# Squares of x written over the raw weight tiles, and two early loads of x issued from ScalarE's queue, in a one-core decoder step

## The chip, the cores and the metric

The kernel runs on one core of a Trainium2 chip. The time is the device time of one execution in microseconds (us); lower is better. A profile is one further execution, recorded by the hardware profiler. Its engines are called PE (TensorE, matmuls), PEld (PE's weight loads), DVE (VectorE), ACT (ScalarE), POOL (GpSimd) and SP (SyncE, which here only issues DMAs). "SPq" and "ACTq" are the sequencers of SP and ACT when they issue a DMA. L12 is line 12 of the kernel as it stood before the change.

## What is computed

One layer of a decoder, for 256 new prompt tokens and 8 x 4 sample tokens, which the kernel puts side by side as T = 288 columns. All data is 32-bit floating point.

```python
def trunk_layer(x, hist_conv, hist_pool, pos0, norm1_g, w_in, b_in, conv_w, conv_b,
                ln_g, ln_b, pool_w, pool_scale, w_out, norm2_g, w_ff1, w_ff2):
    h = rmsnorm(x, norm1_g)
    proj = jnp.einsum("btd,de->bte", h, w_in) + b_in
    a, gate, z = proj[..., :D_CONV], proj[..., D_CONV:2 * D_CONV], proj[..., 2 * D_CONV:]
    u = a * jax.nn.sigmoid(gate)
    ...
    c = jax.nn.silu(layernorm(depthwise_causal_conv(u_ext, conv_w, conv_b), ln_g, ln_b))
    ...
    d = multiscale_pool(z_ext, pos0)
    p = jnp.einsum("btgc,gce->btge", d, pool_w).reshape(bsz, T, D_POOL) * pool_scale
    x = x + jnp.einsum("btm,md->btd", jnp.concatenate([c, p], axis=-1), w_out)
    h2 = rmsnorm(x, norm2_g)
    f = jnp.square(jax.nn.relu(jnp.einsum("btd,df->btf", h2, w_ff1)))
    x = x + jnp.einsum("btf,fd->btd", f, w_ff2)
    return x, u_ext[:, -(CONV_W - 1):], z_ext[:, -(POOL_MAX - 1):]
```

The model width is 2048 (16 blocks of 128 channels), the hidden width of the MLP 8192, the convolution has 31 taps, the pooling windows are 2, 4, 8 and 16. A last rmsnorm follows. The change concerns the first rmsnorm and the first columns of the input projection.

## The kernel before the change

Channels lie on the 128 partitions and tokens along the free axis. x is the tile `xT`, 16 blocks of 128 x 288. Each 32-bit operand of a matmul is split into a high part (a rounded copy, made on ACT) and a low part (what is left, by a subtraction on DVE or POOL), and each product is three matmuls: high by high, high by low, low by high. Weights arrive as raw tiles of 128 x 1024 elements (512 KB); ACT copies one to `whi` (L250, in the first phase L339), and the subtraction gives `wlo` (L251, L340).

The raw tiles come from a pool of six buffers (L87). A tile's buffer goes to a later tile only when everything that reads or writes the earlier one is done. The first eight raw tiles (`first_raw`, L164) serve the first phase; all later ones are loaded by `load` (L154 to L162).

**The first phase** (L323 to L357) runs c from 0 to 7. Step c takes the channel blocks 2c and 2c+1 of x and the raw tile `first_raw[c]`, which holds these two blocks' weights for four groups of 128 output columns. ACT scales the blocks by the norm's gain (`hh`, L332), DVE makes the low part `hl` (L333), ACT and DVE split the weights (L339, L340), and PE does 24 matmuls into four accumulators (L346). c = 0 and c = 1 are done in two halves, one block each, so that they can begin with less data. The norm itself is left out of these products: its factor is a number per token, and is multiplied in behind them.

That factor needs the sum over channels of the squares of x. `square(c)` (L313) has ACT square the two blocks of step c and DVE add the result to a running sum (L318). Before the change the squares lie in a region of the tile `uz` that the pooled inputs `z` need only later. The code calls `square(c - 1)` at the end of step c for c = 1 to 6, and `square(6)`, `square(7)` and the last fold `tot` (L354) in the midst of step 7. Then PE adds over the channels (`token_sum`, L225), ACT takes a square root (L232) and loads the next function table (L208), DVE finishes the reciprocal, PE spreads it over the partitions (L242), and DVE copies it to `rb` (L360).

**Then** comes the next group of columns: 16 k-blocks by two accumulators, three matmuls each (L257 to L259), with four raw tiles of its own, whose low parts are made on POOL (L251). All later groups of the kernel have this form.

**The order of the work.** The program's text says what depends on what; which instruction stands where in each engine's own order is chosen by a planner when the program is built (L632). It may place an instruction ahead of others that come before it in the text. On the chip each engine then runs its instructions strictly in that order. The DMAs of the start are written out by hand (L177 to L196): the small `vec` on ACT, all others on SP, pieces of x and of weights in turn. SP waits where a load's buffer is not free yet, or where the load eight places earlier has not landed.

Of the kernel before, what the change touches and what calls it, by code (L numbers as in the profile page):

```python
# [12 lines left out]
ALU = mybir.AluOpType  # L13
# [7 lines left out]
T = SEQ + NB * NS  # L21
# [8 lines left out]
N8 = DC // P  # L30
# [4 lines left out]
UL = UO + NB * US  # L35
# [46 lines left out]
def trunk_kernel(ctx: ExitStack, tc: tile.TileContext, io):  # L82
    nc = tc.nc
# [14 lines left out]
    def nm(s):  # L98
        seen[s] = seen.get(s, 0) + 1
        return f"{s}{seen[s]}"  # L100
# [8 lines left out]
    def row(name):  # L109
        return rowp.tile([P, T], F32, name=nm(name), tag="row")  # L110
# [4 lines left out]
    def act(name, **kw):  # L115
        return slot(name, F32R, **(kw or {"tag": "act"}))

    def tmp(name, n=T, tag="tmp", bufs=6):
        return tmpp.tile([P, n], F32, name=nm(name), tag=tag, bufs=bufs)
# [10 lines left out]
    def f32(t):  # L130
        return t[:].bitcast(F32)
# [8 lines left out]
    xT = const.tile([P, KT, T], F32, name="xT")  # L140
    uz = const.tile([P, N8 * (UL + ZL)], F32, name="uz")
    u_all = uz[:, 0 : N8 * UL].rearrange("p (k t) -> p k t", t=UL)
    z_all = uz[:, N8 * UL :].rearrange("p (k t) -> p k t", t=ZL)
    squares = uz[:, N8 * UL : N8 * UL + 8 * T].rearrange("p (n k t) -> p n k t", k=2, t=T)

    def v(key, j):
        return vec[:, OFF[key] + j : OFF[key] + j + 1]
# [3 lines left out]
    def raw_tile():  # L151
        return wraw.tile([P, 4, 256], F32, name=nm("wr"), tag="wr")
# [10 lines left out]

    first_raw = [raw_tile() for _ in range(8)]  # L164

    def load_x(k, n):

        nc.sync.dma_start(xT[:, k : k + n, :], io["xT"][:, k : k + n, :])

    def load_first(c, k0=0, k1=2):  # L170

        to = first_raw[c][:].rearrange("p (b k) n -> p b k n", b=2)
        src = io["w"][2 * (c // 4) : 2 * (c // 4) + 2].rearrange("b p k n -> p b k n")
        at = 2 * (c % 4)
        nc.sync.dma_start(to[:, :, k0:k1, :], src[:, :, at + k0 : at + k1, :])

    nc.scalar.dma_start(vec[:, 0:CWO], io["vec"][:, 0:CWO])  # L177
    load_x(0, 1)
    load_first(0, 0, 1)
    load_x(1, 1)  # L180
    load_first(0, 1, 2)
    load_x(2, 2)
    load_first(1, 0, 1)
    load_first(1, 1, 2)
    load_x(4, 2)
# [36 lines left out]
    def token_sum(pt, t, first=True, last=True):  # L222

        for j in range(3):
            nc.tensor.matmul(pt[:TB, j : j + 1], t[:, j * TB : (j + 1) * TB], ones[:, 0:1], start=first and j == 0, stop=last and j == 2)  # L225
# [86 lines left out]

    def square(c):  # L313

        to = squares[:, 0] if c == 0 else squares[:, 1 + c % 3]
        nc.scalar.activation(to, xT[:, 2 * c : 2 * c + 2, :], AF.Square)  # L316
        if c:
            nc.vector.tensor_tensor(squares[:, 0], squares[:, 0], to, op=ALU.add)  # L318

    def lhs(t, k, m):  # L320
        return t[:, 2 * (m // 2) + k, (m % 2) * P : (m % 2 + 1) * P]

    for c in range(8):  # L323
        pair = []
        hi = wspl.tile([P, 4, 256], F32R, name=nm("whi"), tag="whi")
        lo = wspl.tile([P, 4, 256], F32R, name=nm("wlo"), tag="wlo")
        views = [t[:].rearrange("p (b k) n -> p b k n", b=2) for t in (first_raw[c], hi, lo)]
        steps = ((0, 1), (1, 2)) if c < 2 else ((0, 2),)
        for k0, k1 in steps:
            for k in range(2 * c + k0, 2 * c + k1):  # L330
                hh, hl = act("hh"), act("hl")
                nc.scalar.activation(hh, xT[:, k, :], AF.Copy, scale=v("norm1_g", k))  # L332
                nc.vector.scalar_tensor_tensor(out=hl, in0=xT[:, k, :], scalar=v("norm1_g", k), in1=f32(hh), op0=ALU.mult, op1=ALU.subtract)  # L333
                pair.append((hh, hl))
            if len(steps) == 2:
                r, h, l = [t[:, :, k0, :] for t in views]
            else:
                r, h, l = first_raw[c], hi, lo
            nc.scalar.copy(h, r)  # L339
            nc.vector.tensor_tensor(l, r, h.bitcast(F32) if len(steps) == 2 else f32(hi), op=ALU.subtract)  # L340
            for w, x in ((hi, 0), (hi, 1), (lo, 0)):
                if c == 7 and w is lo:
                    token_sum(total, rows[0])
                for k in range(k0, k1):
                    for m in range(4):
                        nc.tensor.matmul(  # L346
                            first_banks[m][:, :T], lhs(w, k, m), pair[k][x],
                            start=c == 0 and k == 0 and w is hi and x == 0, stop=c == 7 and k == 1 and w is lo,
                        )
                if c == 7 and w is hi and x == 0:  # L350
                    square(6)
                    square(7)
                    rows = [row("tot")]
                    nc.vector.tensor_tensor(rows[0], squares[:, 0, 0], squares[:, 0, 1], op=ALU.add)  # L354
        hx += pair
        if 0 < c < 7:
            square(c - 1)  # L357
    ready.extend(itertools.islice(weights, 1))
    rb = row("rb")
# [156 lines left out]
    for g in range(8):  # L516
        bk = bank2()
        gemm(bk, mixc)
        for m in range(2):
            k = 2 * g + m  # L520
# [18 lines left out]
    for ch in range(DFF // FCH):  # L539
        fx = []  # L540
        for g in range(FCH // 256):
# [4 lines left out]
            for m in range(2):  # L546
                t = tmp("t")
# [98 lines left out]
```

## Time and profile before

| | |
|---|---|
| three runs | 1082.31, 1082.53, 1083.08 us; median 1082.53 |
| the profiled execution | 1082.96 us, of which the program's span is 1081.2 |
| PE busy | 1066.8 us, 99% of the span |
| DVE, ACT, POOL busy | 630.5, 470.7, 162.6 us |
| granted TensorE clock, mean | 0.995 of full |
| read from HBM | 181.49 MB, 172 GB/s with the writes |

Each number of the table but the runs comes from the profile page, the execution's own time from its result. PE overlaps its matmuls, so that a busy PE need not be a PE at its peak. In rows of time, the first number is the start in us from the span's beginning and the second the length; "x4" counts instructions that were drawn together, and a bracket gives the idle time of that engine before the row and what ended it. In rows of a DMA, the last number is the time in us from issue to landing.

### The profile page before, as it was taken

Reading aid. Unit: us, or ns where it says so; the run is one execution under the profiler, and the core shown is the slowest. Engines: PE = TensorE matmul, PEld = TensorE weight load, DVE = VectorE, ACT = ScalarE, POOL = GpSimd, SP = SyncE. Lnnn points to the kernel's source line nnn. Section 1 sums busy time; section 2 is a strip of 40 time slices with the busy share of each in tenths; the row PEclk is TensorE's granted clock in tenths of the full one; section 3 lists DMA queues with packets and bytes.
Section 4 is the critical chain, followed back from the end, with each engine's and each line's share of the span. In section 5 each row is a group of like instructions: output and inputs, shape, how many; then the busy total and the mean of one; then the engine's idle time right before and its main releaser. Section 6 shows DMA issues by size and latency. Waiting matters only on the chain.

```text
span 1081.2 us, 19737 instructions
## 1 busy us (share of the span) xinstructions
PE 1066.8 (99%) x8186; PEld 1065.2 (99%) x8186; DVE 630.5 (58%) x982; ACT 470.7 (44%) x650; POOL 162.6 (15%) x108
## 2 busy tenths in 40 slices
PE   9999999999999999999999999999999999999995
PEld 9999999999999999999999999999999999999995
DVE  7799999687555444445455444455444455555453
ACT  7543554575544433334443333444433334444441
POOL 0899878500000000000000000000000000000000
PEclk9999999999999999999999999999999999999997
DMA  9755567555555555555555555555555555555522
GB/s 333 229 185 173 182 169 234 170 168 166 164 167 173 166 169 175 166 167 175 163 170 175 166 167 174 165 169 175 166 167 174 164 170 176 164 168 175 163 93 88
DMA packets 56649, 187.04 MB, mean 173 GB/s; under 512 B 5872, under 2 KB 11504, under 8 KB 56560
## 3 DMA queue, kind: packets, MB, share of 16 engines
q1 hardware_dynamic: 56416, 185.74, 54.8%
q8 instruction: 64, 1.05, 0.4%
q14 instruction: 25, 0.20, 0.1%
q10 hardware_dynamic: 144, 0.05, 0.0%
HBM read 181.49 MB, written 4.28 MB: 172 GB/s over the span
## 4 chain that ended last, share of the span: by engine, by line
PE 98%; DVE 1%; ACT 0%; DMA 0%; SPq 0%; DVEq 0%; issue 0%
PE ac L257 32%; PE ac L258 32%; PE ac L259 32%; PE ac L346 1%; PE cv L346 1%; DVE xT L586 0%; DMA xT<-in_xT 0%; PE pr L242 0%; ACT hh L332 0%; ACT uz L316 0%; PE pf L225 0%; ACT whi L339 0%; DVEq L632 0%; PE m L259 0%; PE m L258 0%
## 5 line engine op out<-in xcount | busy, mean ns | idle before, releaser
L250 ACT CAST whi<-wr 128x1024 fp32r<-128x1024 f32 x330 | 344.9, 1046 | 569.4 <-PE ac L258 542.6
L251 DVE TENSOR_TENSOR wlo<-wr,whi 128x1024 fp32r<-128x1024 f32 x272 | 333.2, 1225 | 366.1 <-ACT whi L250 366.1
L257 PE MATMUL ac<-ah,whi 128*128 128x288 f32 x1024 | 298.7, 292 | 0.0
L257 PE MATMUL ac<-fh,whi 128*128 128x288 f32 x1024 | 298.6, 292 | 0.0
L258 PE MATMUL ac<-al,whi 128*128 128x288 f32 x1024 | 298.5, 292 | 0.0
L259 PE MATMUL ac<-ah,wlo 128*128 128x288 f32 x1024 | 298.5, 291 | 0.0
L258 PE MATMUL ac<-fl,whi 128*128 128x288 f32 x1024 | 298.5, 291 | 0.0
L259 PE MATMUL ac<-fh,wlo 128*128 128x288 f32 x1024 | 298.5, 291 | 0.0
L257 PEld LDWEIGHTS ac<-ah,whi 128*128 128x128 f32 x1024 | 191.9, 187 | 0.0
L258 PEld LDWEIGHTS ac<-al,whi 128*128 128x128 f32 x1024 | 191.9, 187 | 0.0
L257 PEld LDWEIGHTS ac<-fh,whi 128*128 128x128 f32 x1024 | 191.9, 187 | 0.0
L258 PEld LDWEIGHTS ac<-fl,whi 128*128 128x128 f32 x1024 | 191.9, 187 | 0.0
L259 PEld LDWEIGHTS ac<-ah,wlo 128*128 128x128 f32 x1024 | 191.9, 187 | 0.0
L259 PEld LDWEIGHTS ac<-fh,wlo 128*128 128x128 f32 x1024 | 191.9, 187 | 0.0
L251 POOL TENSOR_TENSOR wlo<-wr,whi 128x1024 fp32r<-128x1024 f32 x58 | 138.3, 2403 | 21.3 <-ACT whi L250 19.5
L399 DVE SCALAR_TENSOR_TENSOR pc<-uz,vec,pc 128x256 f32<-128x256 f32 x232 | 98.9, 482 | 6.3 <-ACT pc L388 4.3
L257 PE MATMUL ac<-hh,whi 128*128 128x288 f32 x320 | 92.3, 292 | 0.8 <-ACT uz L420 0.8
L258 PE MATMUL ac<-hl,whi 128*128 128x288 f32 x320 | 92.1, 292 | 0.0
L259 PE MATMUL ac<-hh,wlo 128*128 128x288 f32 x320 | 87.4, 292 | 0.0
L257 PEld LDWEIGHTS ac<-hh,whi 128*128 128x128 f32 x320 | 60.0, 187 | 1.0 <-ACT uz L420 1.0
L258 PEld LDWEIGHTS ac<-hl,whi 128*128 128x128 f32 x320 | 59.9, 187 | 0.0
L259 PEld LDWEIGHTS ac<-hh,wlo 128*128 128x128 f32 x320 | 57.9, 187 | 0.0
(153 smaller groups left out, 872.0 us busy)
## 6 DMA issues: line engine op xcount, KB each, us to landing
wr<-in_w SPq DMA_DIRECT2D x336, 512.0 KB, 3.8
out_u_out<-uz SPq DMA_DIRECT2D x1, 1208.0 KB, 9.0
xT<-in_xT SPq DMA_DIRECT2D x2, 576.0 KB, 8.3
out_yT<-xT SPq DMA_DIRECT2D x2, 576.0 KB, 2.9
uz<-in_hist_c SPq DMA_DIRECT2D x1, 1088.0 KB, 12.3
wr<-in_w SPq DMA_DIRECT2D x4, 256.0 KB, 4.7
xT<-in_xT SPq DMA_DIRECT2D x3, 288.0 KB, 5.9
out_z_out<-uz SPq DMA_DIRECT2D x1, 668.0 KB, 10.2
```

Source lines behind the costliest of these rows:

```text
L250: nc.scalar.copy(hi[:, a:b, :], raw[:, a:b, :])
L251: eng.tensor_tensor(lo[:, a:b, :], raw[:, a:b, :], hi[:, a:b, :].bitcast(F32), op=ALU.subtract)
L257: nc.tensor.matmul(b, wh, xh, start=first, stop=False)
L258: nc.tensor.matmul(b, wh, xl, start=False, stop=False)
L259: nc.tensor.matmul(b, wl, xh, start=False, stop=last)
L346: nc.tensor.matmul(first_banks[m][:, :T], lhs(w, k, m), pair[k][x], start=c == 0 and k == 0 and w is hi and x == 0, stop=c == 7 and k == 1 ...
L399: nc.vector.scalar_tensor_tensor(out=dst, in0=u_all[:, i, w : w + SEQ], scalar=cw[i][:, w : w + 1], in1=pc[i], op0=ALU.mult, op1=ALU.add)
```

## The change

The running sum keeps a place in `uz`, now of 2 x 288 elements. The square of step c is written over the raw weights of step c, into the first 576 of the 1024 elements of `first_raw[c]`. The first square is not added by itself: the first addition takes the squares of c = 0 and c = 1 and writes the sum. The calls stand at the same places, except that `square(0)` takes its own place at the end of step 1. The loads of block 1 and of blocks 2 and 3 of x are issued by ACT in place of SP; their places in the text are the same.

```diff
-    squares = uz[:, N8 * UL : N8 * UL + 8 * T].rearrange("p (n k t) -> p n k t", k=2, t=T)
+    squares = uz[:, N8 * UL : N8 * UL + 2 * T].rearrange("p (k t) -> p k t", t=T)
...
-    def load_x(k, n):
+    def load_x(k, n, eng=nc.sync):
 
-        nc.sync.dma_start(xT[:, k : k + n, :], io["xT"][:, k : k + n, :])
+        eng.dma_start(xT[:, k : k + n, :], io["xT"][:, k : k + n, :])
...
     load_x(0, 1)
     load_first(0, 0, 1)
-    load_x(1, 1)
+    load_x(1, 1, nc.scalar)
     load_first(0, 1, 2)
-    load_x(2, 2)
+    load_x(2, 2, nc.scalar)
     load_first(1, 0, 1)
...
     def square(c):
 
-        to = squares[:, 0] if c == 0 else squares[:, 1 + c % 3]
+        to = first_raw[c][:].rearrange("p a b -> p (a b)")[:, 0 : 2 * T].rearrange("p (k t) -> p k t", t=T)
         nc.scalar.activation(to, xT[:, 2 * c : 2 * c + 2, :], AF.Square)
         if c:
-            nc.vector.tensor_tensor(squares[:, 0], squares[:, 0], to, op=ALU.add)
+            nc.vector.tensor_tensor(squares, first_square if c == 1 else squares, to, op=ALU.add)
+        return to
...
                     rows = [row("tot")]
-                    nc.vector.tensor_tensor(rows[0], squares[:, 0, 0], squares[:, 0, 1], op=ALU.add)
+                    nc.vector.tensor_tensor(rows[0], squares[:, 0], squares[:, 1], op=ALU.add)
         hx += pair
-        if 0 < c < 7:
+        if c == 1:
+            first_square = square(0)
+        elif 1 < c < 7:
             square(c - 1)
```

## The prediction

> **What bounds the kernel now.** I read the span, then the busy time of the engines by stretch, then what TensorE (PE) waits for, then the chain of work that ended last.
>
> ```profile
> span 1081.2 us, 19737 instructions
> ```
> ```profile
> 4.92:9.56 4.64, 3.73 (x26) 3.27 (x25) 2.88 (x6) 3.61 (x8) 0.00 (x0) 1.00 1.02 335
> 9.56:32.26 22.70, 22.69 (x175) 22.52 (x176) 18.73 (x33) 19.75 (x32) 2.00 (x2) 1.00 1.06 383
> ```
> ```profile
> PE pr L242 <- DVE st L239: 1.3, 1, 1.3
> PE warm L213 <- DVE ones L199: 1.1, 1, 1.1
> PE pf L225 <- ACT q L569: 1.0, 1, 1.0
> PE ac L346 <- ACT whi L339: 0.8, 1, 0.8
> PE ac L257 <- ACT uz L420: 0.8, 1, 0.8
> ```
>
> The second fence gives, for each stretch, its length and then PE, weight load, DVE, ACT, POOL, granted clock, DMA share and GB/s. From 9.56 us on PE has no gap in the first phase (22.69 of 22.70). The third fence holds all that PE waits for in the whole span: two waits are in the last norm (L225, L242), one is before the warm-up, one of 0.8 lies in the conv phase, one of 0.8 at the start. So the kernel is bound by PE from about 9.56 us to the last norm. A change that removes no matmul can gain only what PE loses before 9.56, plus that one 0.8.
>
> ```profile
> 1.64 4.28 DMA xT<-in_xT
> 5.95 0.54 ACT hh L332
> 6.48 0.57 ACT uz L316
> 7.06 0.51 ACT whi L339
> 7.57 0.44 ACT hh L332
> 8.00 0.57 ACT uz L316
> 8.58 0.43 ACT hh L332
> 9.00 0.52 ACT whi L339
> 9.56 0.53 PE ac L346 x2
> ```
>
> This is the chain over that start (start, length, what). The second chunk of x (channel block 1) is issued at 1.64 and lands at 5.92. Behind it ScalarE (ACT) scales blocks 1, 2 and 3 (L332), copies raw weights (L339), and does two squares (L316) in between: the squares of blocks 0 to 3, 0.57 us each on the path, although their sum is not needed for another 18 us.
>
> ```profile
> 4.92 0.61 PE L346 MATMUL ac<-hh,whi 128*128 128x288 f32 x2
> ...
> 12.79 0.42 PE L346 MATMUL ac<-hh,whi 128*128 128x288 f32 x2
> ...
> 27.04 0.59 PE L225 MATMUL total<-ones,tot 128*96 128x1 f32 x6
> ...
> 32.84 0.37 PE L257 MATMUL ac<-hh,whi 128*128 128x288 f32 x1
> ```
>
> PE begins c=0 at 4.92 and c=2 at 12.79. Between lie 48 matmuls at 0.13 us (the steady pace: 175 records in 22.69 us, second fence), which is 6.3 us; the stretch took 7.87. So **1.6 us is the most that the start can give**.
>
> **The change, part by part.**
>
> *Squares off the front.* Each square now overwrites the raw tile of its own c, so it must wait until ACT's copy and VectorE's (DVE) subtraction have read that tile. The square of c=0 cannot run before both halves of c=0 are split. The two squares in the chain, 2 x 0.57 = 1.14 us, leave it. Counts do not change: eight squares, seven adds and the fold, on the same engines; they move later. DVE has 18.73 busy of 22.70 and ACT 19.75, so both have room.
>
> *The two loads on ACT's queue.* SP issued them; now ACT does, ahead of its table load.
>
> ```profile
> 1.64 0.47 SPq L168 DMA_DIRECT2D xT<-in_xT  x1
> ...
> 4.64 0.56 SPq L175 DMA_DIRECT2D wr<-in_w  x1
> ```
> ```profile
> 3.39 0.54 ACT L332 ACTIVATE hh<-xT,vec 128x288 fp32r<-128x288 f32 x1 [0.73 <-DMA vec<-in_vec]
> ...
> 11.49 1.05 ACT L339 CAST whi<-wr 128x1024 fp32r<-128x1024 f32 x1
> ```
>
> An issue takes 0.47. Two of them delay ACT by 0.94, and ACT was idle for 0.73 before its first scaling, so that comes 0.2 later, and so does the first matmul: about 5.1. SP is relieved of 2 x 0.5, so each weight load behind is issued 0.5 to 1.0 earlier. Does that help? Only if the DMA engines lacked work:
>
> ```profile
> 3.50:5.00 1.50, 1.50 (x10) 1.50 (x8) 0.89 (x2) 1.05 (x2) 0.00 (x0) 1.00 0.72 150
> 5.00:8.00 3.00, 2.21 (x17) 1.98 (x16) 1.24 (x3) 2.05 (x5) 0.00 (x0) 1.00 1.02 332
> ```
> ```profile
> wr<-in_w SPq DMA_DIRECT2D x1, 512.0 KB, 6.8
> ```
>
> They did, between 3.5 and 5.0: share 0.72, so 0.28 x 1.5 = 0.42 us of idle DMA. From 5.0 on they are full, and nothing is gained by issuing earlier. The last row is the load of c=2's weights, issued at 4.64: it lands 6.8 later, at 11.4, and ACT's cast of it starts at 11.49, at once. **This cast is the new limit.** With the squares gone and x early, PE could reach c=2 at 5.1 + 6.3 = 11.4; but the cast ends 1.05 after the landing. If the landing moves up by the whole 0.42, to 11.0, the cast ends at 12.1 and PE starts c=2 at 12.14 instead of 12.79: **gain 0.65**. If it does not move at all, 12.55: gain 0.24. Both ends are kept. I take the first, because the idle DMA time lies exactly where SP's issues were half a microsecond apart. The 0.2 of the late first matmul and a somewhat later second weight half (x pieces on the other queue now share the engines with it) are hidden behind this same wait: 11.4 stands against 12.14, and that cover of 0.7 is their limit.
>
> [...]
>
> *Later c.* The loads of c=3, 4, 5 come in the same queue and keep the same shift, and their casts stand before PE's need, so the gain of c=2 is kept to the end of the phase.
>
> *Raw tiles held longer.* Six buffers; a tile is free only when its square has been added, some 1 to 3 us later than now, and the loads of c=6, c=7 and of the next group wait for that on SP, with all later loads behind them.
>
> ```profile
> 15.68 8.00 SPq L160 DMA_DIRECT2D wr<-in_w  x4
> ```
> ```profile
> wr<-in_w SPq DMA_DIRECT2D x1, 512.0 KB, 12.2
> ```
>
> The first load of the next group is issued at 15.68 and lands 12.2 later, at 27.9: the chunk of x at the head of the chain needed 4.28, so some 8 of the 12.2 are standing in a full queue, and an issue that comes 3 us later lands at the same time. I cost this at nothing; the cover is those 8 us, and beyond it each microsecond would count.
>
> *The sum of squares comes later.* Now the total stands on PE at 27.04, early, since all squares were done early. After the change the last square waits for DVE's last subtraction.
>
> ```profile
> 25.60 1.22 DVE L340 TENSOR_TENSOR wlo<-wr,whi 128x1024 fp32r<-128x1024 f32 x1
> ```
> ```profile
> 27.67 0.26 ACT L232 ACTIVATE st<-total,eps 96x3 f32<-96x3 f32 x1 [2.22 <-PE total L225]
> ...
> 29.35 3.87 ACT L250 CAST whi<-wr 128x1024 fp32r<-128x1024 f32 x4
> ```
> ```profile
> 30.46 9.48 POOL L251 TENSOR_TENSOR wlo<-wr,whi 128x1024 fp32r<-128x1024 f32 x4 [6.01 <-ACT whi L250]
> ```
>
> That subtraction ends at 26.8; square, add, add and fold put the total at about 29, and on PE it then stands near its place in the code, before the last eight matmuls of c=7, about 30.6. Today the square root, its table and four casts of the next group's weights stand on ACT in this order, and POOL's subtractions (2.4 each) follow. Whether this costs anything depends on ACT's new order, which is fixed when the program is built. The casts need weights that have landed at 27.9, well before a total at 30.6, so I expect at least the first cast ahead of the square root; then POOL has the first low part by 31.5, before PE's need at 32.2, and the cost is nothing.
>
> **Sum.** Profiled execution 1082.96 (span 1081.2 and 1.8 around it) - 0.65 = 1082.3. It lies 0.43 above the median of the runs, 1082.53, so I predict 1081.9.
>
> **Rivals.**
>
> *Slower: the casts stay behind the late square root.* From the total's start at 27.04 today the first cast ends 3.4 later (30.4) and POOL's first low part 5.8 later (32.86). With the total at 30.6 that gives 34.0 and 36.4. PE has done c=7 and the norm's broadcast by about 32.7: it waits 1.3, then for the low part another 0.3 (if sixteen products with the high part come first, 16 x 0.13) to 1.8 (if only four do, as today). That is 1.6 to 3.1, and 1.5 more if the total falls to the very end of c=7: 1.6 to 4.6, less 0.65: 1083.5 to 1086.5, most likely 1084.3. It decides from the point where the total on PE is later than about 29. For it: today's ACT order. Against it: ACT is idle 2.22 before that square root, and the weights are there.
>
> *The landing does not move:* 1082.96 - 0.24 - 0.43 = 1082.3. For it: the DMA engines are full from 5.0 on. Against it: the 0.72. [...]
>
> *More is gained:* the whole 1.6 at the start, and the 0.8 in the conv phase goes with a new order: 1080.2 to 1081.2. Against it: the cast of c=2.
>
> *The squares hold ACT:* a square that waits for DVE keeps the next cast behind it. DVE's subtraction ends more than a microsecond before the next cast in today's order; a few tenths would be lost: 1082.5.
>
> **How the numbers follow.** Forecast 0.50; landing unmoved 0.15; squares hold ACT 0.05; more gained 0.07; casts behind the square root 0.23. The range runs from 1081.0 to 1084.6, which leaves out the upper third of the slower case and a part of the best one. About 0.2% (2.2 us) is what a measurement of this kernel can tell from no change. Faster than 1080.4 needs nearly the whole of the start and the conv wait: 0.03. Slower than 1084.7 is the upper part of the slower case, with a little for a worse order elsewhere: 0.11. The rest, 0.86, is within.
>
> **What would show it.** Right: no square before 9 us on ACT; x block 1 landing before 5; DMA share near 1 from 3.5 to 5; c=2 on PE at about 12.1, directly behind its cast; no gap at the change from L346 to L257, one or more casts before the square root. Wrong: the DMA share full and c=2's weights still at 11.4; a PE wait of over a microsecond at L242, L257 or L259 near 32 us; the loads of the next group landing later than 28.

## The result, and the profile after

| | before | after |
|---|---|---|
| median of the runs, us | 1082.46 | 1088.77 (1088.63 to 1089.57) |
| ratio to before | | 1.0058, interval 1.0048 to 1.0067 |
| the profiled execution, us | 1082.96 | 1088.79 |
| its span, us | 1081.2 | 1086.8 |
| matmuls of c=2 begin | 12.79 | 14.60 |
| the total on PE | 27.04 | 34.98 |
| `rb` is ready | 33.56 | 40.93 |
| first matmul with `w_out` | 164.98 | 167.81 |
| first matmul with the normed convolution (`mh`) | 216.59 | 221.22 |
| last MLP matmul begins | 1066.95 | 1073.24 |

The kernel before was run beside the changed one again, hence its median of 1082.46. The change is slower by 0.6%. The last row says +6.29 us; what follows that last matmul is 0.7 us shorter, so the span grows by 5.6. The other rows give the three places where the 6.29 arises: **1.6** by the end of the first phase, **1.2** at the total, **3.4** at the norm behind the convolution. In this kernel's later lines the numbers are three higher from L360 on (the copy to `rb` is L363, the taps L402) and one higher in the first phase (casts L340, matmuls L347).

What PE waits for in the whole span, by waiting instruction and releaser (us in total, times, longest):

```profile
PE ac L257 <- ACT mh L503: 1.7, 1, 1.7
PE ac L347 <- ACT whi L340: 1.5, 1, 1.5
...
PE total L225 <- DVE tot L355: 1.0, 1, 1.0
```

All three are new or longer than before; only the second (0.8 before) was in the prediction's list of waits.

**The start.** The timeline of ACT, after (start, length; in brackets the idle time and what ended it):

```profile
1.17 0.97 ACTq L168 DMA_DIRECT2D xT<-in_xT  x2
...
3.58 0.52 ACT L333 ACTIVATE hh<-xT,vec 128x288 fp32r<-128x288 f32 x1
6.11 0.62 ACT L340 CAST whi<-wr 128x512 fp32r<-128x512 f32 x1 [2.02 <-DMA wr<-in_w]
6.64 0.53 ACT L333 ACTIVATE hh<-xT,vec 128x288 fp32r<-128x288 f32 x1
```

Before the change, the same cast:

```profile
3.98 0.62 ACT L339 CAST whi<-wr 128x512 fp32r<-128x512 f32 x1
```

The first scaling is 0.19 later, as forecast. But ACT then waits 2.02 us for the first half of the weights, which had landed by 3.98 before. The two x loads are now issued at 1.17 and 1.66; the first starts at the same instant as that weight half (1.18) and shares its DMA engines: in the first 7 us ACT's queue holds the 16 engines for 27.4% of their time, beside 41.6% for SP's (2.9% and 64.7% before). And x gains little: the DMA summary of the first 7 us gives 4.7 us to landing for block 1, so 1.17 + 4.7 = 5.9, against 1.64 + 4.28 = 5.92 before.

```profile
wr<-in_w SPq DMA_DIRECT2D x4, 256.0 KB, 6.2
...
xT<-in_xT ACTq DMA_DIRECT2D x1, 144.0 KB, 4.7
```

Before, the first of these rows read 4.7 for the weight halves. Next, PE after the change:

```profile
3.77 1.49 PE L213 MATMUL warm<-ones 128*128 128x128 f32 x6
6.78 0.85 PE L347 MATMUL ac<-hh,whi 128*128 128x288 f32 x2 [1.52 <-ACT whi L340]
7.43 0.68 PE L347 MATMUL cv<-hh,whi 128*128 128x288 f32 x2
...
9.35 0.68 PE L347 MATMUL cv<-hh,wlo 128*128 128x288 f32 x2
9.83 0.51 PE L347 MATMUL ac<-hh,whi 128*128 128x288 f32 x2
10.18 0.42 PE L347 MATMUL cv<-hh,whi 128*128 128x288 f32 x2
```

The first product comes 1.86 late. The next pairs follow each other every 0.48 us until 9.83, then every 0.26: behind its pause of 1.5 us PE runs twelve matmuls at half pace. It didn't lose its full pace in the pause; it hadn't had it yet. The warm-up matmuls of the first row start every 0.213 us, in both kernels; in e7 below sixteen of them take 2.88, where 16 x 0.213 would be 3.4. The trace's records of the granted clock begin, with full speed, at 10.02 us here and at 5.14 before. The clock column of the windows gives 1.00 for a stretch ahead of the first record, and so doesn't show the half pace.

**The total.** PE, then DVE and POOL around it:

```profile
33.71 0.29 PE L258 MATMUL ac<-hl,whi 128*128 128x288 f32 x1
34.98 0.67 PE L225 MATMUL total<-ones,tot 128*96 128x1 f32 x6 [0.98 <-DVE tot L355]
```
```profile
28.73 0.75 DVE L318 TENSOR_TENSOR uz<-uz,wr 128x576 f32<-128x576 f32 x1
29.73 2.63 DVE L318 TENSOR_TENSOR uz<-uz,wr 128x576 f32<-128x576 f32 x1 [0.25 <-ACT wr L316]
32.40 2.53 DVE L355 TENSOR_TENSOR tot<-uz 128x288 f32<-128x288 f32 x1
```
```profile
29.20 5.42 POOL L251 TENSOR_TENSOR wlo<-wr,whi 128x1024 fp32r<-128x1024 f32 x2 [26.88 <-ACT whi L250]
```

The last two rows of DVE are the surprise: the same addition that takes 0.75 at 28.73 takes 2.63 a microsecond later, and the fold takes 2.53, where before it took 0.46. Both stand exactly beside POOL's two subtractions (29.20 to 34.61), and each ends shortly after one of them.

The squares were late besides. SP, after and before:

```profile
11.22 0.69 SPq L196 DMA_DIRECT2D uz<-in_hist_c  x1
13.12 2.93 SPq L175 DMA_DIRECT2D wr<-in_w  x2
```
```profile
11.55 1.78 SPq L175 DMA_DIRECT2D wr<-in_w  x2
14.25 0.68 SPq L196 DMA_DIRECT2D uz<-in_hist_c  x1
```

The two L175 loads are the weights of c=6 and c=7. Their buffers come free later, and the planner let `hist_c` (1088 KB) go ahead of them. So the cast of c=6 starts later, and behind a wait:

```profile
25.15 1.05 ACT L340 CAST whi<-wr 128x1024 fp32r<-128x1024 f32 x1 [2.21 <-DMA wr<-in_w]
...
28.08 1.03 ACT L250 CAST whi<-wr 128x1024 fp32r<-128x1024 f32 x1
29.02 0.68 ACT L316 ACTIVATE wr<-xT 128x576 f32<-128x576 f32 x1
29.60 1.98 ACT L250 CAST whi<-wr 128x1024 fp32r<-128x1024 f32 x2
32.48 1.05 ACT L250 CAST whi<-wr 128x1024 fp32r<-128x1024 f32 x1 [0.90 <-PE cv L347]
35.69 0.26 ACT L232 ACTIVATE st<-total,eps 96x3 f32<-96x3 f32 x1 [2.17 <-PE total L225]
```

The cast of c=6, the first row here, started at 22.15 before. The four L250 casts do stand ahead of the square root, as the forecast had it.

**The norm behind the convolution.** `rb` is 7.4 us later. Everything that uses it, the gates and the taps of the convolution, follows. POOL around the last addition to `sum_c`, after and before:

```profile
196.33 0.82 POOL L407 TENSOR_TENSOR sum_c<-sum_c,c 128x288 f32<-128x288 f32 x1
197.13 2.40 POOL L251 TENSOR_TENSOR wlo<-wr,whi 128x1024 fp32r<-128x1024 f32 x1
199.49 0.81 POOL L407 TENSOR_TENSOR sum_c<-sum_c,c 128x288 f32<-128x288 f32 x1
```
```profile
193.59 0.81 POOL L404 TENSOR_TENSOR sum_c<-sum_c,c 128x288 f32<-128x288 f32 x1
```

The sum ends at 200.3 instead of 194.4. From there to the end of ACT's first `mh` the chain takes 21 us in both (215.35 - 194.4; 221.17 - 200.3), while PE works through the rest of 384 matmuls with `w_out`. ACT's first `mh` and the last of those matmuls, before:

```profile
214.91 0.43 ACT L500 CAST mh<-cc 128x288 fp32r<-128x288 f32 x1
216.46 0.29 PE L259 MATMUL ac<-ph,wlo 128*128 128x288 f32 x1
```

and after:

```profile
220.74 0.43 ACT L503 CAST mh<-cc 128x288 fp32r<-128x288 f32 x1
218.62 0.29 PE L259 MATMUL ac<-ph,wlo 128*128 128x288 f32 x1
```

Before, the last of them started 1.1 us after `mh` was ready; after, 2.5 us ahead of it. The equal 21 us are a coincidence: after, the averages stand 13.0 us ahead of the sum of squares `pt` on PE instead of 10.9, and the broadcast `pr` follows its reciprocal by 0.3 us instead of 2.2. Windows of after, columns as in the prediction's second fence:

```profile
214.00:222.00 8.00, 6.33 (x50) 6.06 (x49) 5.59 (x14) 5.32 (x8) 0.00 (x0) 0.98 0.51 159
222.00:230.00 8.00, 8.00 (x52) 8.00 (x52) 5.04 (x13) 6.67 (x15) 0.00 (x0) 0.81 0.20 66
```

PE waits 1.7, and then does 52 matmuls in 8 us where it did 64 before: the clock is halved for 3.41 us from 221.64. 1.7 + 3.41/2 = 3.4.

### The profile page after: what moved, and what is told of

It is laid out like the page before. It is cut to its first block, busy times and chain, and to the rows that moved or that the text cites. A ratio compares the mean times of both kernels' runs of the same rounds, so it can differ in the third digit from the quotient of the medians.

```text
span 1086.8 us, 19725 instructions
## 1 busy us (share of the span) xinstructions
PE 1069.1 (98%) x8186; PEld 1067.5 (98%) x8186; DVE 633.8 (58%) x982; ACT 470.9 (43%) x650; POOL 163.5 (15%) x108
## 3 DMA queue, kind: packets, MB, share of 16 engines
HBM read 181.49 MB, written 4.28 MB: 171 GB/s over the span
## 4 chain that ended last, share of the span: by engine, by line
PE 86%; DVE 1%; ACT 0%; DVEq 0%; issue 0%
PE ac L257 29%; PE ac L258 28%; PE ac L259 28%; DVE xT L589 0%; PE pr L242 0%; PE pf L225 0%; DVEq L635 0%; ACT cc L502 0%; PE m L259 0%; PE m L258 0%; PE m L257 0%; PE pmean L480 0%; DVE n L499 0%; DVE xT L566 0%; ACT q L572 0%
## 5 line engine op out<-in xcount | busy, mean ns | idle before, releaser
L250 ACT CAST whi<-wr 128x1024 fp32r<-128x1024 f32 x330 | 344.9, 1046 | 572.0 <-PE ac L258 546.2
L402 DVE SCALAR_TENSOR_TENSOR pc<-uz,vec,pc 128x256 f32<-128x256 f32 x232 | 97.7, 484 | 2.9 <-ACT pc L391 2.3
```

Source lines behind the costliest of these rows:

```text
L250: nc.scalar.copy(hi[:, a:b, :], raw[:, a:b, :])
L402: nc.vector.scalar_tensor_tensor(out=dst, in0=u_all[:, i, w : w + SEQ], scalar=cw[i][:, w : w + 1], in1=pc[i], op0=ALU.mult, op1=ALU.add)
```

## The experiments

The theory from the two traces: the start's loss is the two x loads' alone (shared DMA engines, then PE's half pace); the total is late by the order of the loads and by DVE standing beside POOL; and the norm's loss is due to the late `rb`. The rivals: that the squares make the whole loss and the queue is harmless; that the held raw tiles alone, or POOL alone, make the total late; and that the norm's wait is a matter of its own place in the order, whatever `rb` does. "Last MLP matmul" below is against 1066.95 of before. It is read from one profiled execution of each kernel, which can lie at an end of its runs: e1's is the slowest of ten, those of e2, e5 and e11 are the fastest of theirs. The medians of before beside the runs were 1082.7 to 1083.0.

**The x loads alone**, the squares as before.

```diff
...
-    load_x(1, 1)
+    load_x(1, 1, nc.scalar)
...
-    load_x(2, 2)
+    load_x(2, 2, nc.scalar)
```

> Kernel before, with only the two loads of x moved to ScalarE's queue; the squares stay in uz. Theory A (three losses that add up: 1.5 us at the start from the queue, 1.3 us at the total and 3.5 us at the norm behind the convolution, both from the late squares): the first weight half lands near 6.1 us instead of 3.95, the first real matmul comes at 6.8, the first matmuls run at half pace, c=2 starts near 14.6; total and rb come with it and no wait appears at the total or at the norm: time 1.2 to 2.2 us above before (1083.7 to 1084.7). Theory B (the queue is harmless, the squares cost all): within 0.4 us of before. Theory C (the late start alone sets off the rest): over 4 us above before.

1083.91, ratio 1.0008 (0.9998 to 1.0017); last MLP matmul +1.7. The first cast starts at 5.70 and the first product at 6.37, a little ahead of the changed kernel's, and c=2 at 14.65, within 0.1 of it; no wait is added after the start. The ratio alone can't be told from no change; the trace shows that the start's loss belongs to these two loads.

**The squares alone**, the changed kernel with its loads on SP.

> Changed kernel with the two loads of x back on SP; the squares still overwrite the raw tiles. Theory A: the start is that of before or 0.2 to 0.6 us better (c=2 near 12.2 to 12.6); the last adds and the fold on VectorE still take about 2.5 us each beside POOL; TensorE waits 1.5 to 2.5 us for the total, rb comes at about 39 to 40 us, and the norm behind the convolution waits and falls to half clock: 4 to 6 us above before (1086.5 to 1088.5). Theory B: 6 to 6.5 us above before, all of the change's loss. Theory C: within 0.5 us of before.

1089.46, ratio 1.0063 (1.0047 to 1.0078); last MLP matmul +5.9. The first product is back at 4.92, yet c=2 begins at 13.04, not earlier than before. (The start of e3 below, the fairer one to set it against, has 13.20.) PE waits 1.7 at the total and 1.7 at the norm. Nearly all of the loss is the squares'; the parts don't add (1.7 + 5.9 against 6.3), because what PE loses at the start it need not wait for at the total.

**`rb` late, nothing else**: before, with the copy to `rb` made 21 times.

```diff
-    nc.vector.tensor_copy(rb, rsqrt_rows(total, 1.0 / D, AF.Sigmoid)[:, :T])
+    pr_x = rsqrt_rows(total, 1.0 / D, AF.Sigmoid)
+    for _ in range(21):
+        nc.vector.tensor_copy(rb, pr_x[:, :T])
```

> Kernel before, in which the copy of the norm's factor into rb is repeated 20 more times on VectorE (from PSUM, 0.37 us each): rb comes about 7.4 us later, as in the changed kernel, and nothing else of the first phase changes. If the late rb is what makes TensorE wait at the norm behind the convolution: no new wait before 190 us, then a wait of 1 to 3 us near 215 us with half the granted clock for about 3.4 us behind it, 2.5 to 5 us above before. If that wait comes from something else in the changed order: within 0.5 us of before.

1097.38, ratio 1.0128 (1.0110 to 1.0146). `rb` comes at 43.59, 10 us late, and the last MLP matmul 14.2 late. The direction was right and the size far too small: the norm now waits at three steps, and the clock falls with them (a mean of 0.58 from 218 to 234). A wait of 1.4 at 47.2 us, for the gates, is new as well and was not expected. The planner's order changed with the late `rb`: the norm's broadcast `pr` stands behind all 384 matmuls with `w_out`, as in the changed kernel, and not behind 361 as before.

```profile
PE pt L225 <- DVE ssc L488: 3.7, 1, 3.7
PE pr L242 <- DVE st L239: 3.4, 2, 2.1
PE ac L257 <- ACT mh L502: 2.0, 1, 2.0
```
```profile
218.00:234.00 16.00, 8.68 (x37) 8.35 (x38) 10.20 (x26) 10.13 (x23) 0.00 (x0) 0.58 0.20 68
```

**Two squares in the raw tiles**: before, with only c=0 and c=1 over the raw weights.

```diff
...
-        to = squares[:, 0] if c == 0 else squares[:, 1 + c % 3]
+        to = raw_squares(c) if c < 2 else squares[:, 1 + c % 3]
...
-            nc.vector.tensor_tensor(squares[:, 0], squares[:, 0], to, op=ALU.add)
+            nc.vector.tensor_tensor(squares[:, 0], raw_squares(0) if c == 1 else squares[:, 0], to, op=ALU.add)
```

> Kernel before, in which only the squares of c=0 and c=1 are written over their raw tiles and so leave the chain at the start; the other six stay in uz and run early; all loads on SP. If the squares were 1.14 us of the starting chain and the landing of the weights of c=2 (11.4 us) is the next limit: the first phase gains 0.2 to 0.6 us, total and rb stay as early as before: 1081.8 to 1082.3. If even two late squares push the total back: above 1083.

1083.38, ratio 1.0005 (0.9995 to 1.0014); c=2 begins at 13.36, the total is at 28.83, `rb` at 34.83. Moving just the two squares of the forecast's chain wins nothing either: the square of c=0 stands at 8.67 on ACT and that of c=1 at 11.71, both still ahead of the cast of c=2 (12.28).

A start has to be set against one with the same landings. In e3 ACT does the same work in the same order as before up to 17 us, and still c=2 begins at 13.20 instead of 12.79, because block 1 of x and the second weight half landed at 6.13 and 7.12 in that execution, and at 5.92 and 6.60 in the profile of before. In e4 they landed at 6.41 and 7.08.

**`hist_c` held back** (the squares alone, with that load issued at c=3).

```diff
...
-    nc.sync.dma_start(u_all[:, :, UO:UL], io["hist_c"])
...
+        if c == 3:
+            nc.vector.tensor_copy(u_all[:, 0, UO : UO + 1], hi[:, 0, 0:1].bitcast(F32))
+            nc.sync.dma_start(u_all[:, :, UO:UL], io["hist_c"])
```

> Kernel of e2 (squares over the raw tiles, x on SP) with the load of the convolution's history held back until c=3 has been split, so that it no longer goes ahead of the weight loads of c=6 and c=7 on SP. Theory D (the total is late because that 1.1 MB load overtook two weight loads that were waiting for a raw tile): the weights of c=6 and c=7 land near 22 and 23.5 us again instead of 25 and 26.4, the last adds run before POOL's first subtraction, the total is on TensorE by 31, no wait for it, rb before 36, no wait at the norm: within 0.7 us of before (1081.8 to 1083.2). Theory E (late by the squares' order itself): the weights land early, but the adds still stand behind the last subtraction and beside POOL, total at 33 or later: over 1085.

1089.63, ratio 1.0062 (1.0047 to 1.0077): no gain. The weights of c=6 and c=7 land at 22.4 and 23.7 again, the total stands on PE at 32.47 instead of 34.45 (e2), and the wait at it is gone. But the last two additions still take 3.63 together, beside POOL, `rb` is still at 38.98, and the norm's wait is 2.8. The time that was expected for this case, within 0.7 of before, was missed.

**No POOL beside** (the squares alone, the next group's low parts on DVE).

```diff
-                yield halves([split(raw, G) for _ in range(2) for raw in load()])
+                yield halves([split(raw, V if i == 2 and kind == "conv" else G) for _ in range(2) for raw in load()])
```

> Kernel of e2 with the low parts of the next group's four weight tiles made on VectorE instead of POOL. If VectorE's last add and fold (2.6 and 2.5 us each in e2, 0.75 and 0.46 before) were long because POOL was running a subtraction at the time: they take 0.75 and 0.46 again, and the total comes up to 3.9 us earlier, less the subtractions of 1.2 us each that may now stand before them: total at 31 to 33.5 instead of 34.5, time 1 to 5 us below e2. If they are long for another reason (the raw tiles as operands): 2.5 us each as in e2.

1094.55, ratio 1.0109 (1.0089 to 1.0130): slower. The fold ends at 33.23, 1.2 earlier than in e2, but PE's order has the total only at 36.16, and `rb` comes at 42.28. The time missed, but the question is answered:

```profile
30.98 0.75 DVE L318 TENSOR_TENSOR uz<-uz,wr 128x576 f32<-128x576 f32 x1
31.65 1.22 DVE L251 TENSOR_TENSOR wlo<-wr,whi 128x1024 fp32r<-128x1024 f32 x1
32.78 0.45 DVE L355 TENSOR_TENSOR tot<-uz 128x288 f32<-128x288 f32 x1
```

With POOL idle until 33.29, the last addition takes 0.75 and the fold 0.45. The 2.6 and 2.5 were POOL's doing.

**A warm PE.** Fourteen warm-up steps in place of nine fill PE's idle time at the start; once with the x loads alone (e7), once with the whole change (e9).

```diff
-    for j in range(9):
+    for j in range(14):
```

> Kernel of e1 (only the queue changed) with 14 instead of 9 warm-up matmuls, so that TensorE has no idle time between warm-up and first real matmul. If the queue's loss is mostly TensorE at half pace after idling: the first twelve matmuls take 1.6 us instead of 2.9, c=2 starts near 13.3 instead of 14.65, and the time falls by 1.1 to 1.5 us against e1, to within 0.4 of before. If the loss is the landing of the data itself: no change against e1.

> Changed kernel with 14 instead of 9 warm-up matmuls. The start gets back about 1.3 us as in e7 (c=2 near 13.3 instead of 14.6). If the losses overlap, because the total comes from VectorE at the same time whatever TensorE does: the wait for the total grows by what the start gained, rb and the norm stay, and the time is that of the changed kernel within 0.5 us or worse. If they add up: 1.1 to 1.5 us below the changed kernel.

With the loads alone: 1083.47, ratio 1.0006 (0.9996 to 1.0015). c=2 begins at 13.32 instead of 14.65, though the first product is later:

```profile
3.77 2.88 PE L213 MATMUL warm<-ones 128*128 128x128 f32 x16
6.61 0.53 PE L346 MATMUL ac<-hh,whi 128*128 128x288 f32 x2
6.98 0.42 PE L346 MATMUL cv<-hh,whi 128*128 128x288 f32 x2
```

PE's pairs follow each other every 0.26 us from 6.98 to 8.02 and from 8.90 on; in e1 it was 0.48 from 7.02 to 10.38. So of the 1.8 us lost by c=2, 1.3 are the half pace, and the rest is landing, part of it chance (e3 had 13.20). The time fell less than expected: 0.4 against e1 by the medians, 1.0 by the last MLP matmuls of the two profiles, where 1.1 to 1.5 was forecast. With the whole change: 1089.1, ratio 1.0056 (1.0036 to 1.0076), no gain. c=2 is 1.2 earlier, and the wait at the total grows from 1.0 to 1.7, the rest going in a wait before c=6: PE only arrives earlier at a total that is late for its own reasons.

**Fewer taps**: the changed kernel with 5 of the convolution's 31 taps left out in each block, so that DVE reaches the norm earlier.

```diff
-            for w in range(1, CW):
+            for w in [*range(1, CW - 5), CW - 1]:
```

> Changed kernel with 5 of the 30 taps on VectorE left out in each of the 8 channel blocks of the convolution (40 instructions, about 16 us of VectorE). If the late rb costs at the norm because VectorE is full from rb to the last tap: the wait of 1.7 us at the norm and the half clock behind it go, the rest stays, the last matmul of the MLP ends 3 to 4 us earlier than in the changed kernel (1084.5 to 1086). If the wait comes from the order of instructions at the norm: it stays and the time is that of the changed kernel within 1 us.

1085.38, ratio 1.0023 (1.0011 to 1.0035), 3.4 below the changed kernel. The norm's wait is gone, though `rb` comes at 41.94:

```profile
200.00:222.00 22.00, 22.00 (x175) 22.00 (x174) 15.22 (x34) 15.68 (x26) 8.16 (x4) 1.00 0.53 172
```

From the first matmul with `w_out` to the last of the MLP it takes 901.85 us, as long as before (901.97) and 3.6 less than the changed kernel (905.43). The rest did not stay as expected: in its profile c=2 began at 13.47, near the 13.32 that e7 had at full pace, and the total cost a wait of 1.4. Against the changed kernel e8 is 1.1 ahead at c=2 and 1.0 behind at the first matmul with `w_out`. Of these 2.1 the longer wait is 0.4; the other 1.7 would be a half clock of 3.41 us, by the author's estimate. That the medians differ by about the norm's share is in part luck. The planner moved `pr` too, to behind 290 matmuls, so this run doesn't part the taps from PE's order.

**Only blocks 2 and 3 of x on ACT's queue.**

> Kernel before with only the third load of x (blocks 2 and 3) on ScalarE's queue. If any x load on the second queue holds back the first weight half: it lands after 5 us and TensorE starts late as in e1. If only a load that is issued beside it at 1.2 us does, it does so here as well, since this load is now issued at 1.2 and is twice as long; block 1, issued at 1.64 on SP, then lands later than in before (5.9): c=2 after 13.5, 0.5 to 2 us above before.

1084.52, ratio 1.0013 (1.0003 to 1.0024). One moved load is enough: the first product is at 6.78, c=2 at 14.49.

**Two squares later, raw tiles free**: before, with the squares of c=0 and c=1 held until c=2 is split, still written into `uz`.

```diff
...
+        if c == 2:
+            nc.vector.tensor_copy(squares[:, 0:3:2, 0, 0:1], lo[:, 0:3:2, 0:1].bitcast(F32))
+            square(0)
-        if 0 < c < 7:
+        if 1 < c < 7:
```

> Kernel before with the squares of c=0 and c=1 held back, in uz, until c=2 has been split (by a copy of two columns that they must wait for); raw tiles are free as early as before, all loads on SP. Start: no square before 10 us on ScalarE, c=2 on TensorE at 12.5 to 12.9. If the early total matters as the theory says: the order built for it has the total after the subtractions, so rb comes at 35 to 38 us, and the norm waits if it is later than about 36: 1082 with rb under 36, 1085 or more with rb over 37.

1088.81, ratio 1.0061 (1.0044 to 1.0078), with times from 1084.96 to 1091.13; the profile is of the lowest. In it the first product is at 4.91 and c=2 at 12.62, the total at 32.71 costs no wait, `rb` is at 38.45, and the norm waits 1.7. So late squares alone, with no tile held longer, bring the norm's wait. What the slower executions lost beyond that has no trace here. Its start is the one that gained: with landings as late as in e3 and e4 (6.36, 7.04), c=2 begins 0.6 and 0.7 earlier than there, directly behind its cast (11.52 to 12.57). So the two squares did cost on ACT's chain, and holding both back behind the split of c=2 takes them out of it; writing them over the raw tiles doesn't.

**The last addition of the norm on DVE**: the changed kernel, with the eighth addition to `sum_c` taken from POOL.

```diff
-                    nc.gpsimd.tensor_tensor(sum_c, sum_c, cs[i], op=ALU.add)
+                    (nc.vector if i == 7 else nc.gpsimd).tensor_tensor(sum_c, sum_c, cs[i], op=ALU.add)
```

> The changed kernel with one instruction moved: the eighth and last addition into sum_c, the convolution's sum over channels, is made by DVE in place of POOL. The first phase is as in the changed kernel. If the norm behind the convolution is late because POOL puts that last addition behind one more of its 2.4 us subtractions than before the change (it ends 2.84 us after the last tap, where it took 0.95), then sum_c ends 1.0 to 2.4 us earlier, the averages on PE (pmean) begin 1.2 to 2.4 earlier, the wait of PE for mh falls from 1.7 to below 0.8, the half clock behind it goes with the wait, and the time is 1.0 to 3.2 us below the changed kernel: 1085.6 to 1087.8. If the place of that addition does not matter, because the taps themselves are what is late (their end moved by 4.0), or because DVE's addition stands behind POOL's subtraction just as long, then the wait stays at 1.4 to 1.8 and the time is 1088.4 to 1089.4.

1089.03, ratio 1.0066 (1.0052 to 1.0079): no gain, a miss. DVE and PE in it:

```profile
197.35 2.25 DVE L407 TENSOR_TENSOR sum_c<-sum_c,c 128x288 f32<-128x288 f32 x1
...
216.37 0.17 DVE L239 RECIPROCAL st<-st 96x3 f32<-96x3 f32 x1 [0.89 <-ACT few L208]
```
```profile
218.37 0.81 PE L242 MATMUL pr<-ident,st 96*128 96x96 f32 x6
...
220.84 0.90 PE L257 MATMUL ac<-mh,whi 128*128 128x288 f32 x4 [1.51 <-ACT mh L503]
```

The addition, beside POOL again, takes 2.25 and ends 0.7 earlier than POOL's did. The averages come 1.7 earlier, and the reciprocal is done at 216.54, 1.9 earlier. But PE's order has the broadcast `pr` behind 383 of the 384 matmuls with `w_out`, and so it stands until 218.37. In the kernel before the change it stood behind 361. The order of PE, fixed when the program is built, holds back what the data no longer does.

Put together, by when `rb` is ready: 33.56 (before), 34.33 (e7), 34.83 (e4), 35.04 (e10) and 35.36 (e1) bring no wait at the norm; 38.45 (e11), 38.98 (e5), 40.69 (e12), 40.93 (after), 41.07 (e9), 41.96 (e2), 42.28 (e6) and 43.59 (e3) do. Only e8, with its taps left out, has a late `rb` (41.94) and no wait. Somewhere between 35.4 and 38.5 the cover ends. In the first group `pr` stands behind 361 matmuls with `w_out`, in the second behind 383 or 384. No version was faster than the kernel before.

## Why the prediction was wrong, step by step

1. **"So the kernel is bound by PE from about 9.56 us" and "can gain only what PE loses before 9.56, plus that one 0.8".** As a bound on the gain it held. As a map of where a loss could arise it failed: that PE had no gap at the norm hid that the norm had 1.1 us to spare. The slack was in the trace (`mh` at 215.35, last `w_out` matmul at 216.46), and no row of it was read. A further 2.2 lay between the reciprocal (210.70) and the broadcast on PE (212.93).

2. **"The two squares in the chain, 2 x 0.57 = 1.14 us, leave it."** Wrong for this change. The squares moved from between the scalings to between the casts and still stood ahead of the cast of c=2 (e2, e4), so c=2 began at 13.04 and 13.36, where e3, with the squares in their old place and landings like these, had 13.20: no gain that the scatter of the landings would let one see. That they cost something where they stood was right: held back until c=2 is split, they gave 12.62 (e11), near the 12.55 that the prediction had for a landing that doesn't move.

3. **"That cover of 0.7 is their limit"** (late first matmul and late weight half). The sharing of the DMA engines was named and its size missed: the first weight half, of which the step didn't speak, came 2.1 late and the second 1.1, and PE was granted its full pace only at 10.02. The DMA share between 3.5 and 5.0 did rise, from 0.72 to 0.81, and the weights of c=2 landed at 11.21 instead of 11.47: 0.26 of the 0.42. But that was no longer the limit. The cast that the step called the new limit started at 12.18, behind a square, and not at the landing. The rows show the loads of both queues on the same 16 DMA engines (41.6% and 27.4% of their time in the first 7 us): the saved issue time came back as waiting on another transfer.

4. **"I cost this at nothing; the cover is those 8 us"** (raw tiles held longer). It fell by a reordering that the step didn't consider: the waiting loads let 1088 KB past them, and w6 and w7 landed 3 us later. e5 shows it, by undoing it: 2.0 of the total's lateness go, though the time stays. For the loads of the next group, which the step had in view, the cover held: the first landed at 27.70, before at 27.86.

5. **"About 30.6"** for the total. It was 34.98, from step 4 and from DVE's two instructions beside POOL, 1.9 and 2.1 us longer each (e6). In the trace the addition ends 0.6 after POOL's first subtraction (31.75, 32.36), the fold 0.3 after the second (34.61, 34.93); their lengths are 0.75 and 0.45 where POOL is idle (e6). Before, DVE had done both before POOL began. How POOL's subtractions hold them up was not shown.

6. **"I expect at least the first cast ahead of the square root; ... the cost is nothing."** The first half was right: all four casts went ahead. The second was wrong, since it counted only PE's next need of weights, not who waits for `rb`. That is the costliest omission, 3.4 of 6.3: the lateness of `rb` reaches the norm by the taps on DVE (last one 4.0 later) and by POOL, where the last addition falls behind one more 2.4 us subtraction. PE's order of the norm, pushed back with it, keeps the loss even when the data are early again (e12).

7. **The rivals.** The slower one had its place right, a late total, and its mechanism wrong: nothing stood behind the square root. Its dearest case, 1086.5, was still too cheap, and the range stopped at 1084.6. "The landing does not move" and "the squares hold ACT" were too mild by the same omission.

Two things are not settled. How the norm's loss divides between late data and PE's order was not taken apart: e12 moved the one and left the other, and e3 and e8 moved both. In the changed kernel itself the place of `pr` holds back little: the reciprocal is done at 218.48, and `pr` follows at 218.75, right behind the last matmul with `w_out`. But `pt`, whose operand is ready at 213.33, stands on PE at 215.87 (205.38 and 208.10 before). And what in the planner's rules placed `pr` so late was not looked into.

## What to carry to other kernels

A late result costs nothing only if each of its later readers has slack: follow it to the next places where it meets the critical engine, hundreds of microseconds on if need be, and measure the slack there; a wait of zero in the profile says nothing about it. Moving an early side computation to "later, where there is room" puts it beside other engines' work: look at what runs beside it there. When buffers are held longer, ask what else the queue will let past. And set one profile against another only beyond their scatter: identical starts differed by 0.4 us here.

## What the runs showed of the hardware

The granted clock in the traces of the two kernels: before, it is full from 5.14 us and half from 1070.10, 3.15 after the last MLP matmul began; in the changed kernel it is full from 10.02, half from 221.64 for 3.41, full from 225.06, and half from 1078.39, 5.15 after the last MLP matmul began. The stretches at full clock lasted 1064.96 us (before), 211.63 and 853.33 (after), which are 312.0, 62.0 and 250.0 times the 3.413 us of that half clock. What sets this length was not shown.

Of the changed kernel's pauses behind the start, that of 1.7 us at the norm had a half clock behind it, and that of 1.0 at the total had none (1.00 from 34 to 45 us). In the 3.41 us up to the half clock 6 matmuls of 288 columns began; in the 3.41 us from 33.91, with the pause at the total among them, 14 did; without a pause there is room for 26 (3.41 / 0.13). Behind the pause of 1.5 at the norm of e12 the clock's mean was 0.83 from 222 to 230 (0.81 in the changed kernel). In e3, with three waits of 2.0 to 3.7 at the norm, it was 0.58 from 218 to 234. Whether the length of a pause, its place or the number of matmuls around it decides was not shown. By an estimate from these numbers a half clock of 3.41 us costs half of that, 1.7 us, on top of the pause; the 52 matmuls in 8 us instead of 64 are 1.6 at 0.13 each.

The start differs too. With x loads on ACT and nine warm-up steps, c=2 began at 14.60 (the changed kernel), 14.65 (e1) and 14.49 (e10), behind pauses of 1.5, 1.1 and 1.5 us; in e8, behind one of 1.3, it began at 13.47.
